# Four kinds of small VectorE instruction of an attention phase moved to GpSimd or shortened

## The chip, the cores and the metric

One NeuronCore of a Trainium2 chip runs the whole program. The metric is the device time of one execution in microseconds (us); a run's time stands as a median over executions. Five engines have instruction queues of their own: TensorE (PE, its weight loads listed as PEld), VectorE (DVE), ScalarE (ACT), GpSimd (POOL) and SyncE (SP, which here issues nearly all DMAs). SBUF is the on-chip memory of 128 partitions, PSUM the memory that TensorE writes.

## The reference, cut to what matters

One inference step of a two-layer decoder on 2048 prompt tokens and 8 decode samples. Layer 1 is a state-space mixer, layer 2 a stick-breaking attention of 16 heads of 64. Only the second layer's attention over the prompt is touched by the change:

```
z = einsum('bqhd,bkhd->bhqk', q, k) * HEAD_DIM ** -0.5 + bias
mask = k_pos < q_pos
log_1m = where(mask, log_sigmoid(-z), 0)
log_stick = cumsum(log_1m, reverse=True) - log_1m
w = where(mask, exp(log_sigmoid(z) + log_stick), 0)
o = einsum('bhqk,bkhd->bqhd', w, v)
y = (o * silu(zgate)) @ w_out
```

So a weight is s = sigmoid(z), times the product of (1 - s) over all later, unmasked keys. A masked key has s = 0 and 1 - s = 1.

## The kernel before, in words

The program runs in phases. Up to about 1990 us it does the state-space layer, the projections and the decode samples' scores. Then comes `phase_b2`, the attention over the prompt, which is where all edits lie, and last a short tail of output projections (`out_tail`).

`phase_b2` works through units (`plan_b2`). A unit is one head `h`, one tile of 256 queries `m` (its first or second 128 queries are `par` 0 and 1) and one half of the keys (`half`, 1024 each), with `n` key columns, or, where the diagonal crosses a small block, both `par` at once (`par is None`: a pair unit with n of 256 or 512). There are two groups: first m = 0 to 3 for the eight head pairs `hp` (12 units a head pair), then m = 4 to 7 (28 units a head pair; half 1 ahead of half 0, since the product runs from the last key backwards). Per unit:

- `score`: TensorE computes z into PSUM (`psZ`; a masking matmul with `msk` adds -1e30), ScalarE writes the sigmoid to `s`, GpSimd sets a column of `cc` to 1 and computes cc = 1 - s.
- `weigh`, one unit later: VectorE scans `cc` backwards (a running product, in place), then multiplies s by the shifted `cc`. The multiplication is split: VectorE takes the first `own` columns and GpSimd the rest (384 of 1024). For half 1 the product over the whole half, one column, is copied to a tile `car`, which the scan of half 0 takes as its start value (L1478 to 1491).
- `back`, three units later (`LAG`): TensorE transposes s (`psC`), ScalarE copies to `wT`, and every fourth unit or so (`vals`) TensorE multiplies with V into `psO`.
- `gated`, when a query tile is complete, in four steps, one per unit: VectorE multiplies the gate tile `zb` by psO; ScalarE copies `zb` to `yy[:,0]`, rounded to fp32r; the remainder zb - yy[:,0] goes to `yy[:,1]` (L1546); SyncE stores both to `yT`. A buffer half of `yy` is used again two query tiles later.

Beside that, the first half of the phase takes in the decode samples' value pages (`vp` by DMA, `psA` matmuls), and `stage_ahead` splits the output weights of this phase in the same way, a rounded part `w1h` by ScalarE and a remainder `w1l` (L1659), 16 pieces of 128x512. From head pair 4 of the second group the output projections of finished token tiles run in between (`out_tiles`).

All instructions of the four compute engines of this phase are kept in program order (`OrderedCore`; they all show as L57), so a wait on one engine's queue holds all that stands behind it. DMAs on SyncE are placed by a scheduler.

Of the kernel before, what the change touches and what calls it, by code (L numbers as in the profile page):

```python
# [8 lines left out]
FT = mybir.dt.float32  # L9
# [4 lines left out]
OP = mybir.AluOpType  # L14
# [28 lines left out]
def dram(ap, offset, dims):  # L43
    return bass.AP(tensor=ap.tensor, offset=ap.offset + offset, ap=[list(d) for d in dims])
# [27 lines left out]
class Kern:  # L72
# [1344 lines left out]
    def phase_b2(self):  # L1417
        nc = self.nc = OrderedCore(self.tc, self.nc)
# [5 lines left out]
        with ExitStack() as c:  # L1424
# [43 lines left out]
            def weigh(u, s, cc):  # L1468

                hp, m, half, h, par, n = u  # L1470
                own = n - n // 128 * 3 // 8 * 128
                if par is None:
                    for a in range(2):
                        rev = cc[:, a * (n + 1):a * (n + 1) + n][:, ::-1]
                        nc.vector.tensor_tensor_scan(rev, rev, zero.to_broadcast([128, n]), 1.0, OP.mult, OP.add)
                    w, v = s3(s, n), v3(cc, n, 1)
                    if half:
                        for a in range(2):  # L1478
                            carry[h, m, a] = ap.tile([128, 1], FT, tag="car", name="car", bufs=12)
                            nc.vector.tensor_copy(carry[h, m, a], cc[:, a * (n + 1):a * (n + 1) + 1])  # L1480
                    nc.vector.tensor_mul(w[:, :, :own], w[:, :, :own], v[:, :, :own])
                    if own < n:
                        nc.gpsimd.tensor_mul(w[:, :, own:], w[:, :, own:], v[:, :, own:])
                    return
                first = half or m < 4
                rev = cc[:, 0:n + 1][:, ::-1]
                nc.vector.tensor_tensor_scan(rev, rev, zero.to_broadcast([128, n + 1]),
                                             1.0 if first else carry.pop((h, m, par)), OP.mult, OP.add)
                if half:
                    carry[h, m, par] = ap.tile([128, 1], FT, tag="car", name="car", bufs=12)  # L1490
                    nc.vector.tensor_copy(carry[h, m, par], cc[:, 0:1])
                nc.vector.tensor_mul(s[:, :own], s[:, :own], cc[:, 1:own + 1])
                if own < n:
                    nc.gpsimd.tensor_mul(s[:, own:n], s[:, own:n], cc[:, own + 1:n + 1])
# [21 lines left out]
            def vals(u, wt):  # L1516

                hp, m, half, h, par, n = u
                top = m >= 4 and half == 0

                new = not top and (hp, m // 2) not in o_
                if (hp, m // 2) not in o_:
                    o_.clear()
                    o_[hp, m // 2] = self.ps.tile([128, 512], FT, tag="O", name="psO", bufs=1)
                c1 = m % 2 * 256
                o = o_[hp, m // 2][:, c1:c1 + 256]
                v = V[hp, half]
                nk = n // 128
                for kt in range(nk):
                    c0 = 128 if kt == nk - 1 and (half or m < 4) else 0  # L1530
                    for g in range(2):
                        self.mm(o[g * 64:g * 64 + 64, c0:], v[:, kt, g * 64:g * 64 + 64], wt[g][:, kt, c0:],
                                kt == 0 and new, half == 0 and kt == nk - 1)
                if half == 0:
                    rest.append(gated(hp, m, o))

            def gated(hp, m, o):

                zb = zbs.pop((hp, m))
                nc.vector.tensor_mul(zb, zb, o)  # L1540
                yield
                yn[0] ^= 2
                y = yy[:, yn[0]:yn[0] + 2]
                nc.scalar.activation(y[:, 0], zb, AF.Copy)
                yield
                nc.vector.tensor_sub(y[:, 1], zb, y[:, 0].bitcast(FT))  # L1546
                yield
                nc.sync.dma_start(dram(self.yT, hp * 128 * NC1 + m * 256, [[NC1, 128], [D * NC1, 2], [1, 256]]), y.bitcast(FT))

# [32 lines left out]
            zero = self.ps.tile([128, 512], FT, tag="zero", name="zero", bufs=1)[:, 0:1]  # L1582
            nc.vector.memset(zero, 0.0)
            carry, wT, o_, late, zbs, rest = {}, {}, {}, [], {}, []
# [23 lines left out]
            for i, u in enumerate(us):  # L1608
                hp, m, half, h, par, n = u
                if i in first:  # L1610
                    t = zbs[first[i]] = rows.tile([128, 256], FT, tag="zb", name="zb", bufs=3)
                    nc.sync.dma_start(t, self.zbT[hp * 128:hp * 128 + 128, m * 256:m * 256 + 256])
                s, cc = score(u)
                pend.append((u, s))
                loads(i + 1)
                if scored:
                    weigh(*scored)
                scored = u, s, cc
                advance()
                if i < sw:  # L1620
                    c_ = sum(early[:i + 1])
                    share(0, samples, 76, c_, before)
                    share(1, wload, 17, c_, before)
                    if i == sw - 1:
                        flush(samples, wload)
                        c2.close()
                        xp = self.pool(c, "b3x", side="right")
                        self.Gb = xp.tile([128, D], FT, name="Gb")
                        nc.sync.dma_start(self.Gb, dram(self.gD, 9 * D, [[0, 128], [1, D]]))
                        outs = self.out_tiles(xp, tiles)  # L1630
                else:
                    share(2, outs, steps, sum(cols[sw:i + 1]), after)
                if len(pend) > LAG:
                    back(*pend.pop(0))
            weigh(*scored)
            for x in pend:
                back(*x)
# [7 lines left out]
    def stage_ahead(self, slot, w, ncols, c0):  # L1645

        nc = self.nc
        his, los = [[self.wr[slot].tile([128, D], FR, tag=f"{slot}{g}{k}", name=f"{slot}{g}{k}") for k in range(KT)] for g in "hl"]
        self.W[slot] = his, los
        raw = None  # L1650
        for i in range(2 * KT + 1):
            prev = raw
            if i < 2 * KT:
                raw = self.rp.tile([128, 512], FT, tag="wraw", name="wraw")
                nc.sync.dma_start(raw, dram(w, i // 2 * 128 * ncols + c0 + i % 2 * 512, [[ncols, 128], [1, 512]]))
            if prev is not None:
                k, s = (i - 1) // 2, slice((i - 1) % 2 * 512, (i - 1) % 2 * 512 + 512)
                nc.scalar.activation(his[k][:, s], prev, AF.Copy)
                nc.vector.tensor_sub(los[k][:, s], prev, his[k][:, s].bitcast(FT))  # L1659
            yield  # L1660


# [111 lines left out]
```

## Time and profile before

| what | value |
|---|---|
| median of 3 runs | 3255.84 us (3253.69 to 3263.54) |
| the profiled execution | 3252.9 us, its span 3251.2 us |
| PE busy | 2964.9 us, 91% of the span |
| DVE busy | 2346.1 us, 72% |
| ACT busy | 1309.8 us, 40% |
| POOL busy | 1009.0 us, 31% |

The shares are means over phases with different limits. The attention phase is the stretch from 1990 to 3150 us; there the engines' loads differ from these means, and the rows further down are of that stretch. "Idle before" of an instruction is the time in which its engine had nothing to do, with what ended that time. The chain of waits follows the last instruction back to what released it, step by step.

### The profile page before, as it was taken

The page shows a single profiled execution, that of the slowest core. Times are in us where ns is not written, and L with a number is a line of the kernel's source. Part 1 is how long each engine was busy: PE and PEld are TensorE (multiplying, and loading weights), DVE is VectorE, ACT ScalarE, POOL GpSimd, SP SyncE. Part 2 cuts the span into 40 slices and gives each one's busy share as a digit, 9 for nine tenths or more (in the row PEclk, how much of TensorE's full clock was granted, in tenths as well). Part 3 has the DMA queues.
Part 4 walks back from the last instruction along what each step waited for, and adds up shares of the span by engine and source line. Part 5 has one row for each costly group of instructions (what it writes and reads, how often), then busy time and mean ns, then how long its engine had stood idle before and what let it go on. Part 6 is the DMA issues. An engine that isn't in the chain of part 4 may idle for free.

```text
span 3251.2 us, 57125 instructions
## 1 busy us (share of the span) xinstructions
PE 2964.9 (91%) x19352; PEld 2340.5 (72%) x19352; DVE 2346.1 (72%) x4219; ACT 1309.8 (40%) x2954; POOL 1009.0 (31%) x1273
## 2 busy tenths in 40 slices
PE   7899989999999899898699999888899999999998
PEld 4666767778888799898578886555556566666677
DVE  7799998254434556767656545898989989898874
ACT  4422222232222533234323324555556656555541
POOL 1234433000000100000101103555566656665640
PEclk8999999999999899999799999999999999999999
DMA  7433333565543557667666667665766743333234
GB/s 221 137 97 103 101 99 93 159 192 149 149 124 116 184 152 200 191 191 221 200 190 206 195 196 213 200 204 176 220 211 220 222 137 86 109 112 92 81 106 136
DMA packets 498726, 519.52 MB, mean 160 GB/s; under 512 B 57989, under 2 KB 385958, under 8 KB 498242
## 3 DMA queue, kind: packets, MB, share of 16 engines
q1 hardware_dynamic: 493586, 514.46, 53.5%
q8 instruction: 154, 2.52, 0.3%
q10 hardware_dynamic: 4560, 1.35, 0.2%
q14 instruction: 138, 1.13, 0.1%
q0 software_dynamic: 288, 0.06, 0.0%
HBM read 384.97 MB, written 130.75 MB: 159 GB/s over the span
## 4 chain that ended last, share of the span: by engine, by line
PE 35%; DVE 31%; DMA 14%; issue 7%; SPq 4%; ACT 3%; POOL 3%; DVEq 0%; POOLq 0%; ACTq 0%
PE psA L78 13%; DVE cc L57 9%; PE psB L78 6%; DMA kp<-in_cache_k 6%; PE psA L57 4%; PE psZ L57 4%; PE psO L57 3%; PE psC L57 3%; DVE s L57 3%; DVE kp L1275 2%; DMA vp<-in_cache_v 2%; DVE zs L1276 1%; PE psC L78 1%; SPq L1253 1%; SPq L1112 1%
## 5 line engine op out<-in xcount | busy, mean ns | idle before, releaser
L57 ACT ACTIVATE s<-psZ,sbias 128x512 f32<-128x512 f32 (+2 forms) x640 | 375.4, 648 | 240.9 <-issue 120.1
L57 POOL TENSOR_TENSOR s<-s,cc 128x384 f32<-128x384 f32 (+2 forms) x288 | 358.3, 1244 | 203.7 <-DVE cc L57 167.1
L57 POOL TENSOR_SCALAR cc<-s 128x1024 f32<-128x1024 f32 (+3 forms) x320 | 322.9, 1009 | 293.3 <-ACT s L57 275.9
L57 DVE TENSOR_TENSOR_SCAN cc<-cc,zero 128x512 f32<-128x512 f32 (+5 forms) x256 | 355.3, 1408 | 40.7 <-POOL cc L57 40.7
L57 ACT ACTIVATE wT<-psC 128x512 f32<-128x512 f32 (+3 forms) x640 | 311.7, 545 | 172.6 <-PE psC L57 172.2
L57 PE MATMUL psZ<-X,Q 128*128 128x512 f32 (+2 forms) x1280 | 360.5, 401 | 0.8 <-ACT s L57 0.5
L57 PE MATMUL psC<-idf,s 128*128 128x128 f32 x2176 | 311.0, 283 | 54.2 <-ACT wT L57 44.5
L57 PEld LDWEIGHTS psC<-idf,s 128*128 128x128 f32 x2176 | 249.2, 144 | 141.0 <-ACT wT L57 56.9
L57 DVE TENSOR_TENSOR_SCAN cc<-cc,car,zero 128x1025 f32<-128x1025 f32 x128 | 299.8, 2342 | 38.6 <-POOL cc L57 38.5
L1075 POOL TENSOR_TENSOR lo<-h,hi 128x256 fp32r<-128x256 f32 x92 | 78.4, 861 | 782.0 <-ACT hi L1074 671.8
L78 PE MATMUL psA<-hi,w0h 128*128 128x256 f32 (+1 forms) x1024 | 304.6, 297 | 9.3 <-ACT w0h L892 4.1
L1275 DVE TENSOR_TENSOR kp<-kp,qb 128x512 f32<-128x512 f32 x256 | 180.9, 709 | 181.0 <-DMA kp<-in_cache_k 153.2
L78 PE MATMUL psA<-hi,w0l 128*128 128x256 f32 (+1 forms) x1024 | 295.6, 289 | 2.2 <-DVE w0l L893 2.2
L78 PE MATMUL psA<-lo,w0h 128*128 128x256 f32 (+1 forms) x1024 | 295.6, 289 | 0.2 <-DVE lo L871 0.2
L57 DVE TENSOR_TENSOR s<-s,cc 128x640 f32<-128x640 f32 (+2 forms) x320 | 273.9, 856 | 23.9 <-DVE cc L57 0.9
L57 PE MATMUL psO<-wT,V 128*64 128x256 f32 (+1 forms) x2304 | 262.5, 378 | 19.5 <-DVE zb L57 19.5
L57 PEld LDWEIGHTS psZ<-X,Q 128*128 128x128 f32 x1280 | 213.3, 194 | 56.6 <-issue 22.0
L57 PEld LDWEIGHTS psO<-wT,V 128*64 128x64 f32 x2304 | 160.5, 140 | 108.8 <-DVE zb L57 22.7
L78 PEld LDWEIGHTS psA<-hi,w0h 128*128 128x128 f32 x1024 | 201.5, 197 | 11.9 <-ACT w0h L892 4.5
L78 PEld LDWEIGHTS psA<-hi,w0l 128*128 128x128 f32 x1024 | 201.1, 196 | 2.8 <-DVE w0l L893 2.8
L78 PEld LDWEIGHTS psA<-lo,w0h 128*128 128x128 f32 x1024 | 201.4, 197 | 0.8 <-POOL lo L1075 0.5
L1276 DVE TENSOR_REDUCE zs<-kp 128x8 f32<-128x512 f32 x256 | 174.0, 683 | 5.6
(413 smaller groups left out, 6749.3 us busy)
## 6 DMA issues: line engine op xcount, KB each, us to landing
kp<-in_cache_k SPq DMA_DIRECT2D x256, 256.0 KB
vp<-in_cache_v SPq DMA_DIRECT2D x256, 256.0 KB
Q<-qT SPq DMA_DIRECT2D x128, 256.0 KB
x<-x SPq DMA_DIRECT2D x50, 512.0 KB
X<-kT SPq DMA_DIRECT2D x48, 512.0 KB
x<-in_x_prompt SPq DMA_DIRECT2D x32, 512.0 KB
qT<-kq SPq DMA_DIRECT2D x128, 128.0 KB
kT<-kq SPq DMA_DIRECT2D x128, 128.0 KB
```

What stands on the lines that cost most here:

```text
L57: return self.tc.keep_in_program_order(f(*a, **k))
L78: self.nc.tensor.matmul(out, lhsT, rhs, start=start, stop=stop, skip_group_check=True)
L1075: (nc.gpsimd if k % 2 or kept else nc.vector).tensor_sub(lo[:, k, :256], h, hi[:, k, :256].bitcast(FT))
L1112: nc.sync.dma_start(d, o[g * HD:g * HD + HD].bitcast(FT))
L1253: ld, (r,) = nc.values_load_multi_w_load_instructions(self.pt[:, s * NPG + pg:s * NPG + pg + 1], engines=[mybir.EngineType.SP], min_val=0, ...
L1275: nc.vector.tensor_mul(kp, kp, qb)
L1276: nc.vector.tensor_reduce(zs[:, pg, a * 8:a * 8 + 8], kp.rearrange("p (h d) -> p h d", h=8), axis=mybir.AxisListType.X, op=OP.add)
```

## The change

1. In a pair unit the first 128 queries see no key of the last 128 columns: all are masked, cc is 1 there, and the running product stays 1. The scan of that first tile now leaves them out: 128 or 384 columns instead of 256 or 512.
2. The copies of the carries (`car`) are issued to GpSimd.
3. The remainder of the gated output (`yy[:,1]`) is computed by GpSimd.
4. The remainder of the staged output weights (`w1l`) is computed by GpSimd.

```diff
@@ weigh
                     for a in range(2):
-                        rev = cc[:, a * (n + 1):a * (n + 1) + n][:, ::-1]
-                        nc.vector.tensor_tensor_scan(rev, rev, zero.to_broadcast([128, n]), 1.0, OP.mult, OP.add)
+
+                        L = n if a else n - 128
+                        rev = cc[:, a * (n + 1):a * (n + 1) + L][:, ::-1]
+                        nc.vector.tensor_tensor_scan(rev, rev, zero.to_broadcast([128, L]), 1.0, OP.mult, OP.add)
...
-                            nc.vector.tensor_copy(carry[h, m, a], cc[:, a * (n + 1):a * (n + 1) + 1])
+                            nc.gpsimd.tensor_copy(carry[h, m, a], cc[:, a * (n + 1):a * (n + 1) + 1])
...
-                    nc.vector.tensor_copy(carry[h, m, par], cc[:, 0:1])
+                    nc.gpsimd.tensor_copy(carry[h, m, par], cc[:, 0:1])
@@ gated
-                nc.vector.tensor_sub(y[:, 1], zb, y[:, 0].bitcast(FT))
+                nc.gpsimd.tensor_sub(y[:, 1], zb, y[:, 0].bitcast(FT))
@@ stage_ahead
-                nc.vector.tensor_sub(los[k][:, s], prev, his[k][:, s].bitcast(FT))
+                nc.gpsimd.tensor_sub(los[k][:, s], prev, his[k][:, s].bitcast(FT))
```

Where the instructions stand is seen in the built programs. VectorE (DVE), first group, the start of a head pair (`cc` is 1 - s, `s` the weights, `yy` the gated output's parts; the scan is listed as SCALAR_TENSOR_TENSOR), before (-) and after (+):

```order
-L57 SCALAR_TENSOR_TENSOR cc<-cc,zero 128x512 x2
+L57 SCALAR_TENSOR_TENSOR cc<-cc,zero 128x384
+L57 SCALAR_TENSOR_TENSOR cc<-cc,zero 128x512
 L57 TENSOR_TENSOR s<-s,cc 128x2x384
-L57 TENSOR_TENSOR yy<-zb,yy 128x256
-L57 SCALAR_TENSOR_TENSOR cc<-cc,zero 128x256 x2
+L57 SCALAR_TENSOR_TENSOR cc<-cc,zero 128x128
+L57 SCALAR_TENSOR_TENSOR cc<-cc,zero 128x256
 L57 TENSOR_TENSOR s<-s,cc 128x2x256
```

The remainder has left VectorE's queue, and the next scan stands right behind the multiplication; the first scan of each pair is 128 columns shorter.

GpSimd (POOL), first group, the changed program at a head pair's last units (the columns 640 and 768 are units of m = 2):

```order
L57 TENSOR_TENSOR s<-s,cc 128x256
L57 MEMSET cc 128x1
L57 TENSOR_SCALAR cc<-s 128x640
L57 TENSOR_TENSOR s<-s,cc 128x384
L57 TENSOR_TENSOR yy<-zb,yy 128x256
L57 MEMSET cc 128x1
L57 TENSOR_SCALAR cc<-s 128x768
```

Before, the same rows stood there without the one that writes `yy`. It stands behind GpSimd's part of a multiplication, and the next unit's MEMSET and 1 - s stand behind it.

GpSimd (POOL), second group, the changed program in half 1, at a place where all three moved kinds meet:

```order
L57 TENSOR_SCALAR cc<-s 128x640
L57 COPY car<-cc 128x1
L57 TENSOR_TENSOR s<-s,cc 128x256
L57 TENSOR_TENSOR yy<-zb,yy 128x256
L57 TENSOR_TENSOR w1l_24144<-wraw,w1h_24136 128x512
L57 MEMSET cc 128x1
L57 TENSOR_SCALAR cc<-s 128x768
L57 COPY car<-cc 128x1
L57 TENSOR_TENSOR s<-s,cc 128x128
```

The carry's copy stands ahead of GpSimd's multiplication of the same unit, the two remainders behind it; before, none of the three rows COPY, `yy` and `w1l` was on this queue.

## Rows read from the trace of the kernel before

**Rows 1.** Windows: length, busy us of PE, PEld, DVE, ACT, POOL; clock, DMA, GB/s.
```profile
1990.00:2340.00 350.00, 298.05 (x2018) 196.49 (x2017) 313.82 (x324) 202.48 (x446) 198.97 (x293) 0.95 0.66 197
2340.00:2600.00 260.00, 250.91 (x1691) 155.10 (x1692) 240.44 (x233) 158.11 (x311) 167.79 (x218) 0.99 0.71 217
2600.00:2860.00 260.00, 238.40 (x1561) 167.20 (x1560) 235.14 (x259) 154.19 (x308) 158.61 (x207) 0.97 0.38 110
2860.00:3150.00 290.00, 267.02 (x1702) 201.24 (x1700) 255.31 (x296) 160.81 (x324) 177.14 (x223) 0.98 0.34 99
```

**Rows 2.** Chain of waits, shares by line, of the same four stretches in order.
```profile
by line: DVE cc L57 32.4%; issue 14.9%; DVE s L57 7.7%; DVE yy L57 6.7%; ACT s L57 4.5%; DMA vp<-in_cache_v 3.9%; PE psZ L57 3.8%; PE psC L57 3.5%; PE psO L57 3.4%; POOL cc L57 2.6%; PE psA L57 2.2%; POOL s L57 2.2%; DVE zb L57 2.2%; DMA yT
by line: PE psO L57 17.7%; PE psC L57 17.0%; PE psZ L57 16.0%; PE psA L57 14.4%; DMA vp<-in_cache_v 10.1%; DVE cc L57 8.0%; issue 4.1%; DVE s L57 2.7%; SPq L1253 1.7%; POOL cc L57 1.7%; SPq L1260 1.0%; ACT s L57 1.0%; POOL s L57 0.9%; ACT w
by line: DVE cc L57 45.1%; DVE s L57 15.2%; issue 10.2%; DMA vp<-in_cache_v 3.9%; POOL cc L57 3.9%; DVE yy L57 2.8%; POOL s L57 2.5%; PE psZ L57 2.1%; PE psO L57 2.0%; PE psC L57 1.8%; DVE xo L57 1.6%; DVE rst L57 1.6%; PE psA L57 1.5%; POO
by line: PE psA L57 17.6%; PE psO L57 13.3%; DVE cc L57 13.2%; PE psC L57 12.5%; PE psZ L57 11.5%; issue 6.8%; DVE s L57 3.9%; POOL cc L57 3.9%; DVE rst L57 3.1%; POOL s L57 2.3%; ACT s L57 2.1%; DVE xo L57 2.0%; DVE ss L57 1.4%; POOL x L57
```

**Rows 3.** Groups of DVE by form, 1985 to 3150 us: busy, mean ns, idle before.
```profile
L57 DVE TENSOR_TENSOR_SCAN cc<-cc,zero 128x512 f32<-128x512 f32 x64 | 74.4, 1204 | 22.6 <-POOL cc L57 22.6
L57 DVE TENSOR_TENSOR yy<-zb,yy 128x256 fp32r<-128x256 f32 x64 | 58.1, 908 | 2.1 <-ACT yy L57 2.1
L57 DVE TENSOR_TENSOR_SCAN cc<-cc,zero 128x256 f32<-128x256 f32 x64 | 40.1, 667 | 1.6 <-POOL cc L57 1.6
L57 DVE COPY car<-cc 128x1 f32<-128x1 f32 x128 | 18.5, 147 | 2.2
L57 DVE TENSOR_TENSOR w1l<-wraw,w1h 128x512 fp32r<-128x512 f32 x16 | 17.1, 1071 | 0.1
```

**Rows 4.** Lines 1075 and 666: such remainders in earlier phases, ns min/median/max.
```profile
L1075 POOL TENSOR_TENSOR lo<-h,hi x92: 722/740/1302, 1071.0 to 1907.5; 128x256 fp32r<-128x256 f32 x92
L1075 DVE TENSOR_TENSOR lo<-h,hi x36: 402/418/962, 1069.6 to 1505.4; 128x256 fp32r<-128x256 f32 x36
L666 POOL TENSOR_TENSOR wl<-wraw,wh x32: 1264/1378/1620, 28.1 to 586.4; 128x512 fp32r<-128x512 f32 x32
```

**Rows 5.** Timeline of DVE, 2126 to 2136 us: start, length, instruction.
```profile
2132.16 0.83 DVE L57 TENSOR_TENSOR s<-s,cc 128x640 f32<-128x640 f32 x1
2132.91 1.09 DVE L57 TENSOR_TENSOR yy<-zb,yy 128x256 fp32r<-128x256 f32 x1
2133.92 0.41 DVE L57 TENSOR_TENSOR zb<-zb,psO 128x256 f32<-128x256 f32 x1
2134.25 1.48 DVE L57 TENSOR_TENSOR_SCAN cc<-cc,zero 128x641 f32<-128x641 f32 x1
2135.83 0.69 DVE L57 TENSOR_TENSOR s<-s,cc 128x512 f32<-128x512 f32 x1
2136.44 1.75 DVE L57 TENSOR_TENSOR_SCAN cc<-cc,zero 128x769 f32<-128x769 f32 x1
```

**Rows 6.** Timeline of POOL, the same time.
```profile
2132.21 1.50 POOL L57 TENSOR_TENSOR s<-s,cc 128x384 f32<-128x384 f32 x1 [1.12 <-DVE cc L57]
...
2133.72 0.96 POOL L57 TENSOR_SCALAR cc<-s 128x768 f32<-128x768 f32 x1
```

**Rows 7.** Groups of POOL by form, 1985 to 3150 us.
```profile
L57 POOL TENSOR_TENSOR s<-s,cc 128x128 f32<-128x128 f32 x32 | 27.0, 843 | 20.0 <-DVE cc L57 19.8
L57 POOL MEMSET cc<- 128x1 f32 x256 | 24.3, 95 | 1.8 <-DVE s L57 1.8
```

**Rows 8.** Timeline of ACT and of PE behind the multiplication with the gate.
```profile
2134.41 0.42 ACT L57 ACTIVATE yy<-zb 128x256 fp32r<-128x256 f32 x1 [2.98 <-DVE zb L57]
2135.36 1.42 PE L57 MATMUL psC<-idf,s 128*128 128x128 f32 x8 [3.31 <-ACT wT L57]
```

**Rows 9.** Waits, 1990 to 3150 us: total us, times, longest.
```profile
POOL cc L57 <- ACT s L57: 226.8, 152, 6.1
DVE cc L57 <- POOL cc L57: 77.0, 51, 3.0
```

## The prediction

> **What bounds the kernel now.** All edits lie in the attention phase, so I first cut it into stretches and read each engine's busy time [rows 1], then asked the chain of waits who sets the pace in each [rows 2]. From 1990 to 2340 us DVE is busy 313.8 of 350 us and PE 298.1; the chain runs through DVE (scans 32.4%, multiplications 7.7%, the remainder yy 6.7%, the gate zb 2.2%: 49.0% of the stretch). From 2340 to 2600 us the chain runs through PE (psO, psC, psZ and psA together 65%), which is busy 250.9 of 260 us; DVE is busy 240.4, but holds only 10.7% of the chain with scans and multiplications. From 2600 to 2860 us DVE leads again (scans, multiplications and yy 63.1%), with PE at 238.4 of 260. From 2860 to 3150 us PE leads (55% in its four lines), and DVE has about 17%. So DVE and PE take turns, with little between them: what is taken off DVE is worth something for 610 of the phase's 1160 us, and there PE leaves 52 us and 22 us idle. POOL is busy 57%, 65%, 61% and 61% of the four stretches.
>
> **What the edits take from DVE.** The remainder yy: 64 instructions of 908 ns, 58.1 us. The carries' copies: 128 of 147 ns, 18.5 us (the rows' own busy time). The remainder w1l: 16 of 1071 ns, 17.1 us [rows 3]. The scans: 512 columns take 1204 ns and 256 take 667, so a column costs (1204 - 667) / 256 = 2.1 ns and 128 of them 0.27 us. The rows count 64 scans of either size, of which half, the first of each pair, shrink: 64 x 0.27 = 17.2 us. Together 111 us of DVE's 1044.7 us in the phase (the four stretches summed [rows 1]), about a tenth.
>
> Why is yy so dear? An instruction of its form takes DVE 0.42 us elsewhere (median) and POOL 0.74 [rows 4]. In the timeline DVE's yy starts at 2132.91 and ends at 2134.00, while POOL's multiplication ends at 2133.71 [rows 5, 6]: DVE ends 0.29 us behind POOL, as if it had begun in earnest only then. POOL's own multiplication started when DVE's ran, and ended 0.7 us behind it. I read this as the two engines' multiplications and subtractions taking turns. That is an inference; the price that counts is the 908 ns of the row.
>
> **What POOL gets.** For yy I take the 0.74 us median of POOL [rows 4]: 64 x 0.74 = 47 us. For w1l the 1.38 us of the same form [rows 4]: 16 x 1.38 = 22 us. POOL copying one column is in no row. From below the MEMSET of one column bounds it, 0.10 us, from above the 0.84 us of a 128-column multiplication that mostly waits [rows 7]; I take 0.15, near the MEMSET, as both move one column: 128 x 0.15 = 19 us (13 to 108 between the ends; the upper one would by itself make the slower rival below). In all 88 us on POOL's 702.5 us of 1160, so 790 us, or 70% of a phase some 40 us shorter.
>
> Most of that is hidden. POOL's yy stands behind POOL's multiplication, when DVE has gone on to a scan, and what is late next is POOL's 1 - s of the next unit but one. At the tightest place of the first group, from 2132.16 on, POOL would need 1.55 (multiplication, to 2133.71) + 0.74 + 0.10 (MEMSET) + 0.96 = 3.3 us until cc of the 768-column unit is there [rows 4, 6, 7]. DVE, without its yy, needs 0.75 + 0.33 + 1.58 + 0.61 = 3.3 us until that scan [rows 5]. Equal: a loss of 0 to 0.2 us at two such places for each of 16 head pairs. Where w1l joins, POOL is about 1 us late, a few times. I count 3 us in all, as these are the smallest units; in a 1024-column unit DVE's scan is longer. Without this cover, with every added POOL instruction on the path, it is 88 us (the rival below).
>
> The carry is read four or more units later, so the scan's new wait on POOL costs nothing; if POOL fell that far behind it would stop DVE outright. POOL's multiplication behind the copy starts 0.15 us later, but it ends 0.7 us behind DVE's anyway. The yT store now waits for POOL: released 0.74 us behind POOL's multiplication instead of 0.29, so 0.45 us later, on a queue where its place among the page loads moves by at most a few DMAs. ScalarE reuses that half of yy two query tiles later: nothing counted.
>
> **The sum.** On the chain yy has 6.7% of 350 and 2.8% of 260 us, 23.5 + 7.3 = 30.8 us [rows 2]. The other three edits, 52.8 us, are too short to be listed there; DVE's listed work on the chain in its two stretches is 0.49 x 350 + 0.631 x 260 = 336 us, 0.32 of its busy time in the phase, so 0.32 x 52.8 = 17 us. That makes 48 us. Then come the losses. After a gate multiplication ACT, which had waited 2.98 us for it, and PE, which had waited 3.31 us, run a path of their own to the next head pair's first scan [rows 8]; yy removed on DVE beside that path only lengthens DVE's wait. It is one of four yy of each first-group head pair: 8 x 0.9 = 7 us. With POOL's 3 us, 48 - 7 - 3 = 38 us. In the PE-led stretches I count nothing. The profiled execution took 3252.9 us (2.9 us below the median of the runs), so 3252.9 - 38 = 3215 us.
>
> A rule speaks against the change. The Trainium skill, in "GPSIMD Engine Reference", section "Engine selection", sends elementwise work on a tile to VectorE, with GpSimd about twice as slow for two inputs. The trace agrees on the size (0.74 against 0.42 us [rows 4]); by that alone each yy would be a loss of 0.32 us, some 20 us on 64 if both engines' times counted fully, hence the second rival.
>
> **The rivals.** *First, PE takes all.* Next in line behind DVE is PE; if its waits are only slack that DVE's lead hides, the phase stays as long as PE's path: gain of 5 to 15 us, say 3243 us. For it: PE is busy 85 to 97% in each stretch [rows 1], and DVE's 77 us of waiting for cc goes back to POOL waiting 226.8 us for the sigmoids [rows 9], a path that begins on PE. Against it: PE itself is idle for 74 us in DVE's two stretches, and waits there for DVE by way of ACT [rows 8].
>
> *Second, POOL becomes the pace, and the kernel is slower.* The place is 1 - s behind yy and w1l on POOL's queue. If each added instruction delayed the next scan by its whole length, 88 us would come and 48 - 7 = 41 go: 3252.9 + 47 = 3300 us. It decides as soon as POOL's string per unit is longer than DVE's; above they are equal in the smallest units. The break-even is 41 / 88 = 47% of it on the path. For it: in-order queues, and subtractions that take turns with DVE's multiplications. Against it: POOL is idle 30% of the phase even afterwards, and waits 1.12 us ahead of the very multiplication at the tightest place [rows 6].
>
> *Third, more than the chain shows.* DVE's removed work that lies in its two stretches, on the chain or not, is 42 yy (32 in the first, where each of 8 head pairs has four, and some 10 in the other), 38 us, and by share of time 52.8 x 610 / 1160 = 28 us of the rest: 66 us, 3187 us. It needs PE to give up nearly all of its 74 idle us there.
>
> That the change does not do what it says is excluded by the order of the built programs.
>
> **How the numbers follow.** My case, a gain of 20 to 60 us around 38, gets 0.74; the third rival, above 60, 0.04; PE takes all, 0.14; POOL as the pace 0.08. About 0.3%, or 10 us, is what a measurement of this kernel can tell from no change. PE-takes-all lies to about two thirds within that. Faster by more: 0.74 + 0.04 + 0.05 = 0.83; within: 0.09 + 0.01 of POOL's cases = 0.10; slower: 0.07. The range goes from the third rival's 3187 to the first rival's 3243.
>
> **What would show it.** Right: DVE's groups without yy, car and w1l and busy some 110 us less in the phase; the 512-column group replaced in half by 384 columns at about 0.93 us; POOL's yy at 0.7 to 0.8 us; both DVE-led stretches shorter, the first by some 20 us, and PE's share there higher. Wrong: DVE's wait for POOL's cc grown by about what DVE was relieved of, with POOL not waiting for sigmoids ahead of it (POOL is the pace), or with longer waits for sigmoids (PE is); or POOL's yy at 1.2 us and DVE's multiplications longer by the turns.

## The result, and the profile after

The changed kernel takes 3239.3 us (median of 5 runs, 3232.4 to 3241.4) against 3255.8 us before: ratio 0.9942, 95% interval 0.9924 to 0.9960, a gain of 19 us (13 to 25; the ratio goes by all runs, the two medians are 16.5 us apart). The direction was right and the time lies inside the range, but the forecast gain was 38 us. The profiled execution took 3241.4 us, the slowest of the five, 11.5 less than the one before.

The four stretches of the attention phase after the change, columns as in [rows 1]:

```profile
1990.00:2340.00 350.00, 306.50 (x2082) 197.86 (x2084) 290.19 (x286) 208.91 (x462) 233.70 (x351) 0.96 0.71 204
2340.00:2600.00 260.00, 250.56 (x1690) 154.34 (x1685) 222.69 (x173) 155.01 (x306) 179.34 (x273) 0.99 0.72 216
2600.00:2860.00 260.00, 238.24 (x1583) 168.05 (x1583) 230.19 (x211) 156.76 (x313) 179.34 (x267) 0.99 0.37 109
2860.00:3150.00 290.00, 266.66 (x1668) 201.98 (x1665) 236.07 (x243) 155.28 (x313) 182.01 (x266) 0.96 0.33 98
```

DVE's four figures sum to 979.2 us against 1044.7, so 66 us less, not 111. Of the 111, 17 come back in longer multiplications (below); neighbours on DVE overlap by some 0.08 us [rows 5], so that busy time falls by less than the lengths of the rows; and the fixed windows take in some 14 us more of the program. POOL's four sum to 774.4 against 702.5. PE's four hardly move, except in the first stretch, by 8 us.

The groups of DVE by form that answer to [rows 3], and the two multiplications that changed most, 1985 to 3140 us:

```profile
L57 DVE TENSOR_TENSOR s<-s,cc 128x640 f32<-128x640 f32 x192 | 178.5, 930 | 20.0
L57 DVE TENSOR_TENSOR s<-s,cc 128x512 f32<-128x512 f32 x96 | 79.1, 824 | 10.0
...
L57 DVE TENSOR_TENSOR_SCAN cc<-cc,zero 128x512 f32<-128x512 f32 x32 | 38.2, 1194 | 0.0
...
L57 DVE TENSOR_TENSOR_SCAN cc<-cc,zero 128x384 f32<-128x384 f32 x32 | 30.4, 949 | 22.9 <-POOL cc L57 22.9
...
L57 DVE TENSOR_TENSOR_SCAN cc<-cc,zero 128x256 f32<-128x256 f32 x32 | 21.1, 660 | 0.0
L57 DVE TENSOR_TENSOR_SCAN cc<-cc,zero 128x128 f32<-128x128 f32 x32 | 13.3, 417 | 13.5 <-POOL cc L57 13.5
```

The short scans have the forecast size (384 columns in 949 ns; 0.25 us saved in each). The multiplications of 640 and 512 columns took 885 and 739 ns before, 170.0 and 71.0 us in all: DVE gives back 17 us there. What moved, on POOL:

```profile
L57 POOL TENSOR_TENSOR yy<-zb,yy 128x256 fp32r<-128x256 f32 x64 | 46.5, 727 | 5.9 <-ACT yy L57 5.9
L57 POOL COPY car<-cc 128x1 f32<-128x1 f32 x128 | 38.5, 313 | 22.3 <-DVE cc L57 22.2
L57 POOL TENSOR_TENSOR w1l<-wraw,w1h 128x512 fp32r<-128x512 f32 x16 | 20.3, 1272 | 0.0
```

The chain of waits in the first stretch, to set beside the first line of [rows 2]:

```profile
by line: DVE cc L57 15.1%; issue 12.6%; PE psC L57 9.5%; PE psZ L57 8.3%; DMA vp<-in_cache_v 7.4%; PE psO L57 7.4%; PE psA L57 6.8%; POOL s L57 4.9%; POOL cc L57 4.8%; DVE s L57 4.2%; ACT s L57 3.2%; DMA yT<-yy 3.0%; SPq L1253 2.7%; POOL yy
```

The waits that answer to [rows 9]:

```profile
POOL cc L57 <- ACT s L57: 289.8, 150, 48.7
DVE cc L57 <- POOL cc L57: 121.5, 83, 6.0
```

DVE's scans fell from 32.4% of this chain to 15.1%. PE's four lines rose from 12.9 to 32.0%, the value pages (`vp`) from 3.9 to 7.4%, and the yT store stands on it with 3.0%. DVE waits 44 us longer for 1 - s. POOL waits 63 us longer for sigmoids, but 48.7 of that is one wait at the phase's start, which was there before too and then lay outside the window; without it the two are 241 and 227 us.

Where the 11.5 us lie is told by the gate multiplications, one per query tile, 64 of them. Their row before and after:

```profile
L57 DVE TENSOR_TENSOR zb<-zb,psO x64: 406/414/422, 2003.0 to 3146.5; 128x256 f32<-128x256 f32 x64
```

```profile
L57 DVE TENSOR_TENSOR zb<-zb,psO x64: 407/415/424, 2005.7 to 3135.1; 128x256 f32<-128x256 f32 x64
```

From the first to the 32nd, which is the first group, the timelines give 317.8 us before and 306.2 after. From the 33rd on, the second group, it is 794.5 and 791.8 us (the phase begins 2.7 us later). Nearly all of the gain of this pair of executions is in the first group. (A group's length is counted in this way, from one profiled execution, wherever it is given below.)

### The profile page after: what moved, and what is told of

Its sections match the earlier page's. It is cut to its first block, busy times and chain, and to the rows that moved or that the text cites. A ratio compares the mean times of both kernels' runs of the same rounds, so it can differ in the third digit from the quotient of the medians.

```text
span 3239.7 us, 57105 instructions
## 1 busy us (share of the span) xinstructions
PE 2961.2 (91%) x19352; PEld 2331.7 (72%) x19352; DVE 2274.9 (70%) x4011; ACT 1308.0 (40%) x2954; POOL 1075.4 (33%) x1481
## 4 chain that ended last, share of the span: by engine, by line
PE 40%; DVE 24%; DMA 14%; issue 6%; POOL 4%; SPq 4%; ACT 4%; DVEq 0%; ACTq 0%; POOLq 0%
PE psA L78 14%; DVE cc L57 6%; PE psB L78 6%; DMA kp<-in_cache_k 5%; PE psA L57 5%; PE psZ L57 5%; PE psO L57 4%; PE psC L57 4%; DVE kp L1275 2%; DVE s L57 2%; DMA vp<-in_cache_v 2%; POOL cc L57 1%; DVE zs L1276 1%; PE psC L78 1%; SPq L1253 1%
## 5 line engine op out<-in xcount | busy, mean ns | idle before, releaser
L57 DVE TENSOR_TENSOR_SCAN cc<-cc,zero 128x384 f32<-128x384 f32 (+7 forms) x256 | 338.5, 1343 | 70.6 <-POOL cc L57 70.6
L57 POOL TENSOR_TENSOR s<-s,cc 128x384 f32<-128x384 f32 (+2 forms) x288 | 332.7, 1155 | 99.1 <-DVE cc L57 82.6
L57 PE MATMUL psC<-idf,s 128*128 128x128 f32 x2176 | 306.5, 280 | 51.0 <-ACT wT L57 42.0
L57 DVE TENSOR_TENSOR s<-s,cc 128x640 f32<-128x640 f32 (+2 forms) x320 | 291.2, 910 | 33.3
```

What stands on the lines that cost most here:

```text
L57: return self.tc.keep_in_program_order(f(*a, **k))
```

## The experiments

All ratios are against the kernel before, timed beside the run. A, B, B1 and C are theories that the expectations name.

**Each part alone.** Short scan only, remainder yy only, copies only, w1l only; and the whole change with the copies back on DVE:

```diff
-  nc.vector.tensor_copy(carry[h, m, a], ...)   # e3 alone; e5 the reverse
+  nc.gpsimd.tensor_copy(carry[h, m, a], ...)
```

> Only the shorter scan of each pair's first tile; the three moves undone. It takes 17 us from DVE's busy time and puts nothing on POOL. Theory A (PE and its path to the next sigmoids is next in line, POOL's new work is hidden): a part of it, 5 to 8 us faster than before. Theory B (POOL's new work gives back most of what DVE is relieved of): nothing is given back here, so the edit is worth its whole share, 8 to 12 us, half or more of what all four edits gave together.

> Only the gated output's remainder moved to POOL. DVE's group of 58 us goes, POOL gets 64 of 0.73 us. A: the greatest part of the change's gain, 10 to 16 us faster than before. B: at most 5 us, with DVE's multiplications longer by some 10 us in sum, as they take turns with POOL's subtraction.

> Only the carries' copies moved to POOL, where in the changed kernel one took 0.31 us on average and stood ahead of POOL's multiplication, against 0.15 us on DVE. A: within 3 us of before either way. B: 4 to 10 us slower than before, with DVE's wait for POOL's cc grown in the stretches of the second group.

> Only the remainder of the staged weights moved to POOL, 16 of 1.27 us. A: 0 to 4 us faster. B: 0 to 4 us slower, by the 16 places where POOL's next 1 - s comes about a us later.

> The changed kernel with the carries' copies put back on DVE. A (PE's path is next in line, POOL's work is hidden): the same as the changed kernel within 3 us, 17 to 21 us faster than before. B (POOL's work gives back part of the gain): 3 to 6 us faster than the changed kernel, 22 to 26 us faster than before, and DVE's wait for POOL's cc some 10 us less.

| part | ratio | interval | us |
|---|---|---|---|
| short scan (e1) | 0.9967 | 0.9956 to 0.9979 | -10.7 |
| yy on POOL (e2) | 0.9955 | 0.9943 to 0.9968 | -14.7 |
| carries on POOL (e3) | 1.0008 | 0.9997 to 1.0018 | +2.6 |
| w1l on POOL (e4) | 0.9995 | 0.9985 to 1.0005 | -1.6 |
| all but the carries (e5) | 0.9932 | 0.9913 to 0.9952 | -22 |

The four parts sum to 24, which the interval of the whole (13 to 25) allows. The copies gain nothing. The timeline of DVE before shows why:

```profile
2454.26 2.02 DVE L57 TENSOR_TENSOR_SCAN cc<-cc,zero 128x897 f32<-128x897 f32 x1
2456.31 0.15 DVE L57 COPY car<-cc 128x1 f32<-128x1 f32 x1
2456.38 0.82 DVE L57 TENSOR_TENSOR s<-s,cc 128x640 f32<-128x640 f32 x1
```

And the same place of the sequence after, without the copy:

```profile
2116.35 2.02 DVE L57 TENSOR_TENSOR_SCAN cc<-cc,zero 128x897 f32<-128x897 f32 x1 [0.51 <-POOL cc L57]
2118.47 0.83 DVE L57 TENSOR_TENSOR s<-s,cc 128x640 f32<-128x640 f32 x1
```

In both the multiplication starts 0.10 us behind the scan's end: the copy lay in that gap. It is so for all 128 copies: the gap from scan to multiplication is 0.105 us in the median with a copy and 0.104 without. On POOL a copy takes 313 ns in the mean ahead of POOL's part of the multiplication.

**Is PE next in line?** One matmul of the scores (the rounding remainder of the queries, `ql`) is left out of before and of after:

```diff
-  self.mm(zz, ql[:, q], x[:, :n], False, False)
```

> The kernel before with half of the scores' matmuls left out (the pass with the low part of q), so that z is less exact; PE is relieved by some 640 matmuls, about 140 us, and nothing else is changed. A: PE bounds a good part of the phase, so this alone is 30 to 80 us faster than before. B: DVE bounds it, 10 to 30 us faster.

> The changed kernel with the same half of the scores' matmuls left out. What counts is its distance from the run with the kernel before so relieved. A: with PE out of the way the change is worth more, 35 to 70 us. B: POOL and the turns with DVE are untouched by this, so the change is worth the same 15 to 22 us as it is beside the whole of PE's work.

Before: 0.9930 (0.9911 to 0.9950), -23 us. After: 0.9865 (0.9843 to 0.9886), -44 us. With PE relieved the change is worth 21 us (each interval is some 7 us to either side, so 12 to 30), about as much as with PE loaded (19): PE does not take the missing gain as a whole. In the profiled executions the second group gains 10 us then (781.7 to 771.5) instead of 3, but they were e7's slowest and e8's fastest, so that PE holds a part there is not shown.

**What is left in the remainder and the copies.** The remainder left out and the carries' copies too:

```diff
-  nc.gpsimd.tensor_sub(y[:, 1], zb, y[:, 0].bitcast(FT))
-  nc.gpsimd.tensor_copy(carry[h, m, par], cc[:, 0:1])
```

> The changed kernel with the gated output's remainder and the carries' copies left out altogether, on either engine: the stored remainder is zero and every scan of half 0 starts from 1, so the results differ. The weights' remainder stays on POOL. A: POOL's share of the work cost next to nothing, so this gains at most 5 us over the changed kernel, 19 to 25 us faster than before. B: the 85 us that POOL no longer does come back as time, 35 to 45 us faster than before, about what the prediction forecast.

0.9822 (0.9804 to 0.9841), -58 us: 39 us beyond the change. So these small instructions still cost, now from POOL's queue, twice what the change had gained. The next runs ask whether it is their time on POOL (busy two thirds of the phase) or what waits for them.

**The remainder cut to one column, left out, or its time alone.** e9 keeps every wait of the remainder and computes one column. e13 leaves the remainder out and keeps the copies. e14 lets POOL do a subtraction of the same size at the same place on a tile that nobody waits for; `yy[:,1]` stays zero in e13 and e14.

```diff
-  nc.gpsimd.tensor_sub(y[:, 1], zb, y[:, 0].bitcast(FT))
+  nc.gpsimd.tensor_sub(y[:, 1, 0:1], zb[:, 0:1], y[:, 0, 0:1].bitcast(FT))   # e9
+  nc.gpsimd.tensor_sub(cTf, cTf, cTf)                                       # e14
```

> The changed kernel with POOL's remainder of the gated output cut to its first column (the rest of the stored remainder is zero, so y_prompt differs). The instruction stays at its place on POOL's queue, and the gate tile zb and the store of yT still wait for it; only its 0.73 us is gone. Theory B1 (POOL's time is what gives the gain back): nearly all of what leaving it out gave, 45 to 55 us faster than before. Theory C (not its time, but that it comes three units late and is the last to read zb, whose reload holds SyncE's queue, and with it the pages of cached values, until it is done): 19 to 30 us faster than before, near the changed kernel.

> The changed kernel with the gated output's remainder left out altogether (the stored remainder is zero); the carries' copies and the weights' remainder stay on POOL. zb and the yT store then wait for ScalarE's copy alone, one unit earlier. Both theories expect the same, as both causes are gone: 40 to 54 us faster than before. If it is under 30, the carries' copies and the constant start of the scans are what the run with both left out had gained.

> As the run without the remainder, but POOL makes a subtraction of the same 256 columns at the same place, on a tile that nobody else uses, so its time and its turns with DVE stay and nothing waits for it. B1 (POOL's time): 17 to 26 us faster than before, as the changed kernel. C (the waits on it): 38 to 50 us, within 6 us of the run without the remainder.

e9: 0.9926 (0.9910 to 0.9942), -24 us. e13: 0.9828 (0.9814 to 0.9841), -56 us. e14: 0.9836 (0.9823 to 0.9850), -53 us. The row of e14 shows that POOL spent most of the time that the remainder had taken (39.0 us of 46.5):

```profile
L57 POOL TENSOR_TENSOR cT<-cT 128x256 f32<-128x256 f32 x64 | 39.0, 609 | 0.1
```

39 us of POOL cost some 3 us or nothing (the intervals of e13 and e14 overlap); the same place in the queue with next to no time, but with the waits kept, loses 29 us of e14's gain. So POOL's time by itself is nearly free, and what costs is that something waits for the remainder. e6 gained 13 us more than theory B had expected, e13 and e14 2 to 3 us more than theory C. The first group lasts 306.2 us after, 297.0 in e9, and 273.7 and 277.6 in e13 and e14.

Who waits is seen on SyncE's own queue, 1990 to 2340 us (line waited at, releaser, total us, times, longest). Before (L1612 is the load of the gate tile `zb`, L1548 the yT store):

```profile
SPq L1612 <- DVE zb L57: 64.1, 12, 9.5
SPq L1612 <- DVE yy L57: 28.9, 9, 6.2
...
SPq L1548 <- DVE yy L57: 9.8, 6, 2.6
```

After (the same two lines are L1614 and L1550):

```profile
SPq L1614 <- POOL cc L57: 72.7, 18, 7.0
...
SPq L1550 <- POOL cc L57: 9.9, 7, 3.8
SPq L1614 <- ACT yy L57: 5.6, 3, 2.6
SPq L1614 <- POOL yy L57: 3.6, 1, 3.6
```

And e14:

```profile
SPq L1616 <- ACT wT L57: 28.4, 13, 6.2
...
SPq L1550 <- ACT yy L57: 10.0, 4, 3.5
```

The load of a gate tile needs the buffer of the tile three earlier (`bufs=3`), and the remainder is that buffer's last reader. (The releaser is named by a neighbour in its queue: DVE's `zb` or POOL's MEMSET of `cc` stand next behind the remainder.) SyncE keeps order, so while it waits there, the value pages, queries and stores behind it are not issued. Before, it stood 93 us of 350 at this load, after 82, in e14 28; with all smaller rows and the yT store's 105, 93 and 45. The hold was there before the change; the change only handed it from DVE's remainder to POOL's. No run takes the remainder's waits out of the kernel before, so how much of e14's 53 us could be had without the change is not known.

With the remainder's move alone (e2) two waits of the engines grow in this stretch, PE's weight loads for the pages and ACT's wait for the yT store that still reads the half of `yy` it is to overwrite. Before, and then e2:

```profile
PEld psA L57 <- DMA vp<-in_cache_v: 20.0, 20, 2.7
...
ACT yy L57 <- DMA yT<-yy: 10.8, 2, 5.9
```

```profile
PEld psA L57 <- DMA vp<-in_cache_v: 29.8, 22, 3.5
ACT yy L57 <- DMA yT<-yy: 26.1, 5, 8.5
```

**The load later.** The gate tile is asked for at its query tile's last unit instead of its first; the full computation is kept. In e10 after, in e11 before, in e12 after with the copies back on DVE, in e15 with the one-column remainder, in e16 before with only the short scan:

```diff
-            first = {v[0]: k for k, v in qs}
+            first = {v[1]: k for k, v in qs}
```

> The changed kernel with zb's load issued at its query tile's last unit instead of its first, so that its buffer is mostly free by then and SyncE need not wait; POOL's work is unchanged. C: 35 to 50 us faster than before, and SyncE's wait at the zb load in the stretch from 1990 to 2340 us down from some 80 us to under 30. B1: 17 to 23 us faster, as the changed kernel.

> The kernel before with the same later load of zb; none of the change's edits. C: SyncE waited here for some 95 us in the first stretch as well, so this alone is 12 to 30 us faster than before. B1: within 5 us of before.

> The changed kernel with zb's later load and the carries' copies back on DVE. C: 38 to 55 us faster than before, some 3 us better than with the copies on POOL. B1: 20 to 25 us faster.

> The changed kernel with the remainder cut to one column and zb loaded later: C: zb's hold is gone, and what is left of the waits is the yT store's, 38 to 48 us faster than before; B1: 22 to 30, as with one column alone.

> The kernel before with the shorter scans and zb's later load, none of the three moves to POOL. The two parts alone gave 10.7 us each, so 17 to 24 us faster than before if they add. The distance to the changed kernel with the later load (35.5 us) is then what the three moves are worth when zb holds nothing: C: 11 to 18 us; B1: 0 to 10 us.

| load late, with | ratio | interval | us |
|---|---|---|---|
| before (e11) | 0.9967 | 0.9954 to 0.9980 | -10.7 |
| short scan (e16) | 0.9940 | 0.9926 to 0.9953 | -19.5 |
| the change (e10) | 0.9891 | 0.9874 to 0.9907 | -35.5 |
| the change, carries on DVE (e12) | 0.9889 | 0.9871 to 0.9906 | -36 |
| one-column remainder (e15) | 0.9836 | 0.9823 to 0.9850 | -53 |

The late load is worth 10.7 us without the change, and on top of it the change is worth 25 us (e10 against e11) instead of 19. e12, at 3214.2 us, is the fastest kernel of the full computation here (with e10 within its interval), ahead of the kernel before and of the changed one. With the load late, the three moves are worth 16 us beyond the scan (e10 against e16), with it early 8 (after against e1). The first group of e10 lasts 283.0 us; its second, 796.0, gains nothing. The two waits of the engines in the first stretch, after and then e10:

```profile
PEld psA L57 <- DMA vp<-in_cache_v: 31.3, 25, 4.1
...
ACT yy L57 <- DMA yT<-yy: 12.9, 2, 8.7
```

```profile
PEld psA L57 <- DMA vp<-in_cache_v: 13.7, 14, 2.5
...
ACT yy L57 <- DMA yT<-yy: 12.7, 5, 4.3
```

These two rows together are 44.2 us after, 26.4 in e10, 18.9 in e15 and 12.9 in e14, in the order of the times. e9 does not fit (52.0, at a time no worse than after's), nor does e11 (7.5, at 3242 us), so they are a sign of the hold and not its measure.

A sign that was expected did not come. In e10 SyncE was to stand under 30 us at the load, and it stood 43; at the yT store it stood 45 instead of 11 (all rows; the largest):

```profile
SPq L1614 <- POOL cc L57: 41.4, 14, 4.5
SPq L1550 <- POOL cc L57: 40.1, 18, 5.6
...
SPq L1550 <- POOL yy L57: 4.8, 2, 3.5
```

Load and store together are 88 us, against 93 after; in e11 they are 101, against 105 before. So the late load hardly shortens SyncE's waiting for the remainder; it moves about half of it from the load to the store. That other transfers then stand ahead of the hold would fit the pages' shorter waits, but was not followed transfer by transfer. The gate tile itself comes in time: in none of these runs does DVE's gate multiplication wait for it. e11 (10.7 us, 12 to 30 expected) and e12 (36, 38 to 55 expected, and no better than e10) gained less than theory C said, e15 more.

Why one column instead of 256 is worth 18 us with the late load and some 5, within the intervals, with the early one, is not settled. It does show that the remainder's length counts once something waits for its end.

**Both transfers off SyncE's queue, or only written elsewhere.** e17 issues the gate tile's load right behind the remainder, and the yT store too, from POOL's own queue. e18 writes the load at the same place, but leaves both on SyncE.

```diff
                 nc.gpsimd.tensor_sub(y[:, 1], zb, y[:, 0].bitcast(FT))
+                load_zb(nc.gpsimd)     # e18: nc.sync
...
-                nc.sync.dma_start(dram(self.yT, ...), y.bitcast(FT))
+                nc.gpsimd.dma_start(dram(self.yT, ...), y.bitcast(FT))   # e17 alone
```

> The full computation of the changed kernel. The gate tiles' loads and the yT stores leave SyncE's queue for GpSimd's: each load of a gate tile is issued right behind the remainder that last reads its buffer, each store behind its remainder, on the engine that made it, so neither makes anything wait. If SyncE's wait for the remainder (82 us in 1990 to 2340 us in the changed kernel) is what costs, the pages behind it come early and the time falls to about that of the runs that leave the waits out, -50 us or more against before (ratio 0.985 or less), less what GpSimd needs to issue 128 DMAs; the page matmuls' waits for vp in the attention phase fall well below the 79 us of the changed kernel. If instead the late gate tile or the late store itself costs, with the pages only following, the time stays within 8 us of the late load's 0.989. If issuing on GpSimd costs it a microsecond each, the ratio is above 0.994.

> As the run before it, but both kinds of DMA stay on SyncE's queue; only the gate tile's load is written behind the remainder that frees its buffer. SyncE still waits for the remainder ahead of each load and each store. If SyncE's hold is the cost, this is worth about what the late load was (ratio 0.987 to 0.991), clearly behind the run before it; if it is when the gate tile's load is asked for, the two are equal within 0.002.

e17: 0.9929 (0.9907 to 0.9951), -23 us. e18: 0.9972 (0.9961 to 0.9983), -9 us. In e17 the pages come in time (waits in the first stretch):

```profile
ACT yy L57 <- DMA yT<-yy: 22.8, 5, 6.1
PEld psA L57 <- DMA vp<-in_cache_v: 6.1, 8, 1.7
```

And POOL pays for it (groups of POOL, 1985 to 3140 us):

```profile
L57 POOL DMA_DIRECT2D yT<-yy x64 | 49.6, 775 | 1.6 <-issue 1.0 <-POOL yy L57 0.6
L57 POOL DMA_DIRECT2D zb<-zbT x61 | 36.5, 599 | 18.1 <-POOL yy L57 18.1
```

With both transfers off SyncE's queue the pages' wait falls from 31.3 to 6.1 us, so they were held behind these two; the full price of that is not shown. 50 us or more had been expected. That POOL's 86 us of issuing took the rest back is likely, with ACT now waiting 22.8 us for the yT store, but no run tests it by itself. e18 keeps the hold:

```profile
SPq L1557 <- POOL cc L57: 90.8, 28, 7.0
```

That is as much as after at load and store together, and half of the change's gain is gone. It was expected to be worth what the late load was, and is not. Its first group is even shorter than after (299.0 us); the loss is in the second, 808.6 instead of 791.8, in an execution that was the slowest of its twelve. The cause is open.

## Why the prediction was half right

**Who is bound where: right.** DVE led the first stretch [rows 2], and in the profiled executions nearly all the gain is there.

**The sum, term by term.** What each part gained alone, against its term of the sum, in us:

| term | forecast | measured alone |
|---|---|---|
| yy: 31 - 7 (beside PE's path) - 3 (POOL) | 21 | 14.7 (10 to 19) |
| scans, 0.32 of 17.2 | 5.5 | 10.7 (7 to 14) |
| carries, 0.32 of 18.5 | 6 | -2.6 (-6 to 1) |
| w1l, 0.32 of 17.1 | 5.5 | 1.6 (-2 to 5) |

Two steps failed, and the scans' surplus hid a part of it, by luck.

*The first is the common share of 0.32 for three edits at different places.* It gave the carries and w1l 11 us, and neither gained anything measurable. The carries' 18.5 us of rows cost no time, as they lay in a gap that is there anyway: taking them away left DVE's next start where it was. On POOL I took 0.15 us for a copy; it is 0.31 in the mean and 0.18 in the median. For the scans the share was too low; why they weigh more, and why w1l weighs nothing, was not taken apart further.

*The second is in yy: the waits on SyncE's queue, put at nothing.* Its price on DVE was read rightly, and POOL's time was nearly free, as e14 shows. Of the queue the prediction says only that the yT store's "place among the page loads moves by at most a few DMAs". I read the waits of the five engines and never those of SyncE's queue. There the remainder released not only the yT store but the reload of its gate tile, on which SyncE stood 93 us of the first stretch already. A DVE that runs ahead then meets pages and stores that are held: with yy moved alone (e2) PE's wait for the pages grew from 20.0 to 29.8 us and ACT's for the yT store from 10.8 to 26.1.

How much of the missing gain this explains is in part open. The three moves were forecast at 32 us; they are worth 8 beyond the scan, and 16 with the load late. Without any wait for the remainder the whole is 53 (e14), but there the hold that the kernel before has too is gone as well.

**The range.** The time lies inside it near its upper end, 3243 us, which came from the first rival, PE takes all. The runs do not bear that rival out, so the range's holding is no support for the sum.

**The DVE-led third stretch, some 15 us by the same shares: did not come.** The second group took 791.8 us instead of 794.5. There DVE's waiting for 1 - s grew (from 52.5 to 73.5 us, 2340 to 3150 us) and POOL's for sigmoids did not (157.2 and 156.9), which was the sign named for POOL as the pace. For the phase as a whole that rival falls all the same: the kernel is faster, and e14 leaves POOL 39 of its added us and gains 53. What holds the second group is open: without the remainder and the copies it takes 783.4 us (e6), with PE relieved 771.5 (e8).

**The first rival, PE takes all,** is not borne out. PE's lines grew to a third of the chain in the first stretch, but with PE relieved the change is worth no clear more (e7, e8), and in e14, with all of PE's work, PE is busy 323.9 of 350 us there instead of 306.5.

**The third rival** forecast a gain of 66 us if every instruction taken off DVE counted. The phase gives 53 to 58 us once nothing waits on the remainder (e14, e13, e6), but these runs also drop waits that the kernel before had, so they are no proof of that rival.

**The rule on engines.** The prediction set the Trainium skill's rule ("GPSIMD Engine Reference", "Engine selection") against the change: elementwise work goes to VectorE, GpSimd being about twice as slow for two inputs. Elsewhere in the program the trace agrees (0.74 against 0.42 us [rows 4]). In this phase it decides otherwise: yy takes 727 ns on POOL, 908 on DVE, and moving it alone gained 14.7 us.

## What to carry to other kernels

Read the waits of the DMA queue beside those of the engines: a reload that stands early in an in-order queue, waiting for its buffer's last reader, holds every transfer behind it, and an engine that runs ahead then meets transfers that are late. Before moving a small instruction, ask who waits for its result and its buffers. When a reload has to wait, try it at several places: here a later one gained 11 to 17 us, one right behind the buffer's last reader lost 10. A group's busy time is no price: look in the timeline whether the next instruction starts any sooner without it.

## What the runs showed of the hardware

A one-column copy behind a scan is free on DVE: the multiplication starts 0.10 us behind the scan's end with it or without, at all 128 copies, and moving them gained nothing (e3). On POOL the same copy takes 313 ns in the mean.

The prediction's reading that DVE and POOL take turns is borne out by the kernel before. DVE's yy took 0.42 us at the 9 places where POOL was idle as it began, and 0.98 in the mean at the 52 where POOL's multiplication was running.

DVE's multiplications also lengthen when they start beside POOL's 1 - s, which has one tensor input. After the change, on DVE:

```profile
2133.31 0.69 DVE L57 TENSOR_TENSOR s<-s,cc 128x512 f32<-128x512 f32 x1
2133.92 1.48 DVE L57 TENSOR_TENSOR_SCAN cc<-cc,zero 128x641 f32<-128x641 f32 x1
2135.51 1.06 DVE L57 TENSOR_TENSOR s<-s,cc 128x512 f32<-128x512 f32 x1
```

and on POOL at that time:

```profile
2134.47 0.72 POOL L57 TENSOR_TENSOR yy<-zb,yy 128x256 fp32r<-128x256 f32 x1
2135.14 0.09 POOL L57 MEMSET cc<- 128x1 f32 x1
2135.20 0.82 POOL L57 TENSOR_SCALAR cc<-s 128x768 f32<-128x768 f32 x1
2136.00 0.84 POOL L57 TENSOR_TENSOR s<-s,cc 128x128 f32<-128x128 f32 x1
```

The multiplication from 2133.31 takes 0.69 us; the one of equal size from 2135.51, which starts inside POOL's 1 - s (2135.20 to 2136.02), takes 1.06. Over the phase after, the 31 multiplications of 512 columns that start so take 0.98 us in the mean, and the 44 that start with POOL idle 0.69. Of both sizes together, 75 start so after and 39 before; this is most of the 17 us that the multiplications gave back. That the two engines take turns is inferred from such places; no run here took it away by itself.
